# Gate products and two weight sums of the first stage on GpSimd, and a younger head's scalings behind an older head's states

## The chip, the core and the metric

The kernel runs on one core of a Trainium2 chip. Five engines work side by side, each through its own queue in order: TensorE (matrix products, PE in the profile), VectorE (DVE), ScalarE (ACT), GpSimd (POOL) and SyncE (SP, which issues most of the DMAs). GpSimd issues some DMAs itself. An instruction that waits holds up everything behind it on its engine.

The metric is the device time of one execution in microseconds (us): 2118.82 us as the median of three runs of the kernel before (2116.53, 2118.82 and 2120.09).

## What is computed

The reference is a decoder trunk of two layers over 1024 tokens of width 1024. A mixer and a squared-ReLU MLP alternate, each followed by a layer norm. The second layer's mixer is a convolution, which the change does not touch. The first layer's mixer, HGRN2, is a gated linear recurrence with eight heads of 128 channels:

```python
proj = h @ w_in                       # columns [q | forget | value | output gate]
q, fz, v, g = jnp.split(proj, 4, axis=-1)
q = silu(q);  f = lb + (1 - lb) * sigmoid(fz);  k = 1 - f
# per head: S_t = diag(f_t) S_{t-1} + k_t v_t^T ,  o_t = S_t^T q_t
o = o * rsqrt(mean(o * o) + eps) * norm_g
o = o * silu(g)                       # the gate product
mix = o @ w_out
```

## The kernel before

All products are in float32 by splitting each operand into a high part (a rounded copy that ScalarE makes) and a low part (operand less high part, on VectorE), and by three matmuls for high-high, high-low and low-high. The large products use a scheme with seven products of half-size blocks in place of eight (a form of Strassen's), so their operands are sums and differences of blocks. One such product with its operands is called a form here, with the numbers 1, 2, 6, 5, 7, 3, 4 in the order in which they are computed.

**First stage.** After the value columns (up to about 90 us) come the columns of q, forget and gate. They are taken in 12 pairs of 128-column blocks (`PAIRS`, line 37): eight pairs hold q and forget of one head, four hold the gates of two heads. A pair has seven forms, and `pair_product` (line 815) makes each with twelve matmuls in four groups of three. Each group ends with a call of `slot` (line 842), so a form has four slots. `later(n, job)` (line 353) puts a job off by n slots: it is emitted, in the order of its call, when `tick` (line 359) reaches that slot. So the order of the work on every engine is written out by hand by these counts of slots; no scheduler moves anything.

**Weight sums.** `make_form` (line 543) prepares the weight side of one form some four forms ahead of its product. A pair's four weight blocks b0 to b3 (tiles `pr`, of which there are five) are loaded by SP (`load_block`, line 536, DMA at line 541). Four sums of 128x512 make the other operands, in place, all on VectorE: b0 := b0+b2 behind form 2 (line 565), total := b0+b3 in form 6 (line 557), b1 := b1+total in form 6 (line 558, used by form 3), and b2 := b2+b3 in form 5 (line 560, used at once by form 5). `high` (line 570) has ScalarE copy the operand into the tile `fs` (line 571 in the profile), and `low` (line 562) has VectorE make the low part. For forms 6 and 5 the copy is put off by one slot, so that the sum has time (line 574). When a block has been used for the last time its tile is free, and `load_block` issues the next load into it.

**Recurrences.** `recurrence(h)` (line 591) is a generator of eighteen steps for one head; `step` (line 827) advances every active head by one step, older first, about every four slots. Steps 1 to 6 have no matmul: they clamp the forget gate (`f`), multiply cumulative products into q and k (`scale`, line 606, written as qk<-qk,T in the profile), take a reciprocal and make a second copy of k and q with it (`kd`, line 632 on ScalarE and line 634 on VectorE). Steps 7 to 11 form the scores inside chunks of 128, with a scaling and a masked copy put off by one slot behind each. Step 13 transposes k on TensorE, and ScalarE copies it one slot later to `kt` (line 668). Steps 14 and 15 form the outer products of kt and the values; one slot later `chain` (line 718) makes the running states with four small VectorE operations for each half, and `attend` (line 727) of the next step reads them on TensorE. `settle` (line 675) then sums squares, has GpSimd make the root (lines 680 and 474), and steps 17 and 18 transpose the result, scale it and store it to DRAM (line 706, `od`). The next head becomes active when the older one has done nine steps (`LAG`), so steps 1 to 6 of the younger head run beside steps 10 to 15 of the older one.

**Gates.** `gate_turn` (line 851) runs at each slot. It has SP load a head's half from `od` into one of two tiles `u` (line 856), and when the gate of that half is made and the load is nine slots old, VectorE multiplies the two (line 861, t<-u,t in the profile, twelve times; the last two heads are handled by `last_in`, line 904). Two slots later SP stores the product to `zd` (line 864).

**Beside it.** GpSimd's queue in this stage holds the small root operations and `block_sums` (line 368), which prepares weight sums of a later stage in DRAM: per call two plain DMAs (lines 375 and 376), then three accumulating ones (lines 377 and 379), each of which waits for the landing of the one it builds on.

Of the kernel before, what the change touches and what calls it, by code (L numbers as in the profile page):

```python
# [12 lines left out]
ALU = mybir.AluOpType  # L13
# [224 lines left out]
def body(ctx, tc, d, out):  # L238
    nc = tc.nc
# [9 lines left out]
    def view(kb, shape, dt=F32, name="t"):  # L249
        at, top = int(kb * 1024), KBYTES * 1024  # L250
        if at < edge[0]:
            if edge[0] < top:
                space.tile([P, (top - edge[0]) // 4], F32, name="gap")
            edge[0] = 0
        if at > edge[0]:
            space.tile([P, (at - edge[0]) // 4], F32, name="gap")
        edge[0] = at + (prod(shape) + 7) // 8 * 32
        return space.tile([P, *shape], dt, name=name)
# [34 lines left out]
    vector = Clocked(nc.vector, bg.dve, vector_cost)  # L293
# [59 lines left out]
    def later(n, job):  # L353
        if n:
            waiting.append((ticks[0] + n, job))
        else:
            job()
# [175 lines left out]
    total = view(122, wide_t, F32, "total")  # L533
    made, blocks_of, at_block, at_form = [], {}, [0], [0]

    def load_block():
        p, b = divmod(at_block[0], 4)
        if p < len(PAIRS) and free:
            at_block[0] += 1
            raw = blocks_of[p, b] = free.pop(0)  # L540
            nc.sync.dma_start(out=raw, in_=d["wp"][p, b])

    def make_form(wait=1):
        p, i = divmod(at_form[0], 7)
        if p == len(PAIRS):
            return
        at_form[0] += 1
        i, b, s = ORDER[i], [blocks_of.get((p, k)) for k in range(4)], fs()
        hi, lo = s[:, 0], s[:, 1]
        made.append(s)  # L550

        def plus(out, x, y):
            vector.tensor_tensor(out=out, in0=x, in1=y, op=ALU.add)

        raw = total if i == 6 else b[{1: 0, 2: 1, 5: 2, 7: 0, 3: 1, 4: 3}[i]]
        if i == 6:
            plus(total, b[0], b[3])
            plus(b[1], b[1], total)
        elif i == 5:
            plus(b[2], b[2], b[3])  # L560

        def low():
            vector.tensor_tensor(out=lo, in0=raw, in1=hi.bitcast(F32), op=ALU.subtract)
            if i == 2:
                plus(b[0], b[0], b[2])
            if i in (5, 7, 3, 4):
                free.append(raw)
                load_block()

        def high():  # L570
            nc.scalar.copy(out=hi, in_=raw)
            later(wait, low)

        later(wait if i in (6, 5) else 0, high)

    level_ps, out_ps = (banks[:, k : k + 2].rearrange("p k (a b) -> p (k a) b", b=P) for k in (3, 5))
    state_ps = banks[:, 7].rearrange("p (a b) -> p a b", b=P)
# [2 lines left out]
    def mul(o, a, b):  # L580
        vector.tensor_tensor(out=o, in0=a, in1=b, op=ALU.mult)
# [169 lines left out]
    recs, active, pace, alone = [], [], [0.0, 0.0], [False]  # L751
# [75 lines left out]
    def step():  # L827
        if recs and (not active or len(active) == 1 and active[0][2] >= LAG):
            active.append([recs[0], recurrence(recs.pop(0)), 0])
        if not active:  # L830
            return False
        if not (len(active) == 1 and active[0][0] == H - 1 and active[0][2] >= LAG):
            alone[0] = not alone[0]
            if alone[0]:
                return True
        for one in list(active):
            one[2] += 1
            if next(one[1], one) is one:
                active.remove(one)
        return True  # L840

    def slot():
        tick()
        gate_turn()
        pace[0] += pace[1]
        if pace[0] >= 1:
            pace[0] = pace[0] - 1 if step() else 0.0
# [3 lines left out]
    def gate_turn():  # L851
        now = ticks[0]
        if to_load and len(loaded) < 2 and done.get(to_load[0], now) <= now - 7:
            at = to_load.pop(0)
            u = p1("u")
            nc.sync.dma_start(out=u, in_=od[at[0]][at[1]])
            loaded.append((at, u, now))
        if loaded and loaded[0][0] in gates and loaded[0][2] <= now - 9:
            (h, half), u, _ = loaded.pop(0)
            g = gates.pop((h, half))  # L860
            mul(g, u, g)

            def store():
                nc.sync.dma_start(out=zd[half][:, h, :], in_=g)
                stored[h, half] = ticks[0]

            later(2, store)

    oT, ws = [None, None], [[None] * 4, [None] * 4]

# [52 lines left out]
    for _ in range(5):  # L923
        load_block()
    v_products(3, [lambda: cut_v(4, a3), make_form, make_form])
    v_products(4, [make_form])
    fs.views.append(view(160, (2, HT), F32R, "fs"))
# [13 lines left out]
    for i in range(2):  # L941
        load_values(i)

    make_form()
    tick(4)
    for p, (kind, j) in enumerate(PAIRS):
        st = {"banks": dict(turn_of)}
        turn_of = {"z": turn_of["a"], "a": turn_of["b"], "b": turn_of["z"]}
        pace[1] = 0.0 if p == 0 else 0.6 if p < 3 else 0.5
        if kind == "g" and p < len(PAIRS) - 1:  # L950
            to_load += [(2 * j, 0), (2 * j + 1, 1), (2 * j, 1), (2 * j + 1, 0)]
        if p == len(PAIRS) - 1:
            seam()
        for i in ORDER:
            if kind == "q" and i == 2:
                while any(a[0] <= j - 3 for a in active) or recs and recs[0] <= j - 3:
                    tick()
                    step()
            pair_product(p, i, made.pop(0), st)
            later(2, make_form)  # L960
            if (7 * p + ORDER.index(i)) % 6 == 1 and len(to_sum) > 4:
                block_sums(*to_sum.pop(0), gap=12)
        if kind == "q":
            later(4, lambda j=j: recs.append(j))
# [8 lines left out]
    while step():  # L973
        tick()
# [21 lines left out]
    def gain(kb, name, layer):  # L996
        return vec(kb, f"{name}_g", layer), vec(kb + 4, f"{name}_b", layer)
# [75 lines left out]
    g, b = gain(192, "ln_mix", 0)  # L1073
    y = [view(160 + 16 * h, (NTB, D), F32, "y") for h in range(2)]
# [253 lines left out]
    y = [view(32 + 16 * h, (NTB, D), F32, "y") for h in range(2)]  # L1328
    fw = Slots(nc, vector, slots([112, 120, 144, 152, 128, 136, 168], "dw"), raws([192, 196, 200, 204, 160, 164], "dr"), spare, 5, range(12, 56))
    fh = Slots(nc, vector, slots([0, 8, 16, 24, 96, 104, 176], "dh"))  # L1330
    g, b = gain(184, "ln_ffn", 0)
# [236 lines left out]
    y = ct  # L1568
    g, b = gain(120, "ln_ffn", 1)
# [87 lines left out]
```

## Time and profile before

| | us |
|---|---|
| median of three runs | 2118.82 |
| the profiled execution | 2120.82 |
| its span on the core | 2119.0 |
| TensorE busy in the span | 2086.5 |
| VectorE busy | 1447.1 |
| ScalarE busy | 1037.4 |
| GpSimd busy | 390.0 |

The profile is of one execution. Its views are: the page (busy time of each engine over the span); the busy time by windows (a row has the window, its length, the busy us of PE, PE's weight loads, DVE, ACT and POOL with counts of instructions, then the granted TensorE clock as a share of full speed, the DMA share and GB/s); the waits (engine, the tile it was about to write and the line, what released it, us in total, number, longest); the timeline of an engine (start us, us, engine, line, operation, out<-in, shape, count; in brackets the idle time before it and who ended it); groups of instructions (line, engine, operation, tiles, shapes, count | busy us, mean ns | idle us before); and the chain of waits, which follows the work that ended last back through what released each piece. Matmuls and most vector operations are emitted by helper lines and all stand at line 173, so they are told apart by their tiles.

### The profile page before, as it was taken

The page shows a single profiled execution, that of the slowest core. Times are in us where ns is not written, and L with a number is a line of the kernel's source. Part 1 is how long each engine was busy: PE and PEld are TensorE (multiplying, and loading weights), DVE is VectorE, ACT ScalarE, POOL GpSimd, SP SyncE. Part 2 cuts the span into 40 slices and gives each one's busy share as a digit, 9 for nine tenths or more (in the row PEclk, how much of TensorE's full clock was granted, in tenths as well). Part 3 has the DMA queues.
Part 4 walks back from the last instruction along what each step waited for, and adds up shares of the span by engine and source line. Part 5 has one row for each costly group of instructions (what it writes and reads, how often), then busy time and mean ns, then how long its engine had stood idle before and what let it go on. Part 6 is the DMA issues. An engine that isn't in the chain of part 4 may idle for free.

```text
span 2119.0 us, 27037 instructions
## 1 busy us (share of the span) xinstructions
PE 2086.5 (98%) x10056; PEld 1731.7 (82%) x10056; DVE 1447.1 (68%) x1868; ACT 1037.4 (49%) x1593; POOL 390.0 (18%) x384
## 2 busy tenths in 40 slices
PE   8999999999999999999999999999999999999998
PEld 7888787888888888888888888888878888888887
DVE  8697788877775665665666997899436443654456
ACT  5445454541465555544444677378443443433333
POOL 0112212201000000000002897299001000000001
PEclk9999999999999999999999999999999999999999
DMA  4778889771589786989997654564694987855542
GB/s 182 235 176 212 234 226 243 191 257 70 170 256 316 261 280 226 365 327 336 350 335 285 265 193 184 210 256 150 190 334 159 353 308 288 327 204 190 196 161 100
DMA packets 173494, 508.62 MB, mean 240 GB/s; under 512 B 16433, under 2 KB 45361, under 8 KB 172337
## 3 DMA queue, kind: packets, MB, share of 16 engines
q1 hardware_dynamic: 157872, 448.16, 59.0%
q0 software_dynamic: 15488, 58.72, 12.1%
q8 instruction: 79, 1.29, 0.2%
q14 instruction: 55, 0.44, 0.1%
HBM read 377.32 MB, written 196.61 MB: 271 GB/s over the span
## 4 chain that ended last, share of the span: by engine, by line
PE 78%; DVE 9%; DMA 6%; POOL 3%; issue 2%; ACT 2%; SPq 0%; DVEq 0%; POOLq 0%; ACTq 0%
PE ps L173 78%; POOL cb L173 3%; DVE qk L173 2%; DMA wa<-ready 1%; DMA raw<-in_w_dram 1%; DVE t L173 1%; DMA y<-kept 1%; DVE fs L173 1%; DMA vr<-in_wv_dram 1%; DMA hf<-ht 1%; DMA raw<-in_w1q_dram 1%; DVE xf L173 1%; DVE at L173 0%; DMA dh<-hf 0%; DVE vr L173 0%
## 5 line engine op out<-in xcount | busy, mean ns | idle before, releaser
L173 PE MATMUL ps<-dw,dh 128*128 128x512 f32 x2688 | 611.3, 389 | 0.0
L173 PEld LDWEIGHTS ps<-dw,dh 128*128 128x128 f32 x2688 | 504.1, 188 | 104.9 <-ACT dh L70 0.5
L173 PE MATMUL ps<-x1f,fw 128*128 128x512 f32 x1344 | 308.5, 390 | 1.1 <-DVE c L173 0.9
L173 PEld LDWEIGHTS ps<-x1f,fw 128*128 128x128 f32 x1344 | 251.2, 188 | 54.0 <-issue 1.3
L173 PE MATMUL ps<-xa,wa 128*128 128x512 f32 x1152 | 268.8, 392 | 0.0
L173 PE MATMUL ps<-xf,fs 128*128 128x512 f32 x1008 | 251.1, 400 | 1.7 <-ACT t L781 0.8
L173 PEld LDWEIGHTS ps<-xa,wa 128*128 128x128 f32 x1152 | 214.2, 188 | 43.5
L173 POOL TENSOR_TENSOR cb<-cb,prod 128x512 f32<-128x512 f32 x176 | 234.6, 1342 | 17.5 <-ACT prod L1425 7.0
L173 PEld LDWEIGHTS ps<-xf,fs 128*128 128x128 f32 x1008 | 185.6, 190 | 40.2 <-DVE t L173 2.2
L173 DVE TENSOR_TENSOR dh<-dh 128x1024 fp32r<-128x1024 f32 x112 | 136.4, 1222 | 114.5 <-ACT dh L70 113.8
L173 DVE TENSOR_TENSOR dw<-dr,dw 128x1024 fp32r<-128x1024 f32 x112 | 136.6, 1222 | 105.6 <-ACT dw L70 105.0
L173 DVE SCALAR_TENSOR_TENSOR ps<-u,par,ps 128x512 f32<-128x512 f32 x288 | 198.6, 748 | 9.9 <-ACT ps L1437 8.5
L70 ACT CAST dh<-dh 128x1024 fp32r<-128x1024 f32 x112 | 117.0, 1050 | 146.5 <-DMA dh<-hf 146.0
L70 ACT CAST dw<-dr 128x1024 fp32r<-128x1024 f32 x112 | 117.4, 1053 | 135.9 <-PE ps L173 124.5
L173 PE MATMUL ps<-xc,wa 128*128 128x512 f32 x768 | 174.4, 389 | 0.0
L474 POOL TENSOR_TENSOR mv<-mv,nhalf 128x1 f32<-128x1 f32 x32 | 45.2, 1414 | 686.3 <-DVE mv L173 686.3
L173 PEld LDWEIGHTS ps<-xc,wa 128*128 128x128 f32 x768 | 144.1, 188 | 29.9
L1425 ACT ACTIVATE prod<-u,par 128x512 f32<-128x512 f32 x176 | 125.4, 722 | 54.3 <-POOL cb L173 53.7
L173 DVE TENSOR_TENSOR wa<-raw,wa 128x1024 fp32r<-128x1024 f32 x51 | 66.5, 1306 | 67.9 <-ACT wa L70 67.8
L70 ACT CAST wa<-raw 128x1024 fp32r<-128x1024 f32 x51 | 53.6, 1050 | 117.5 <-PE ps L173 109.6
L1288 POOL COPY next<-ss 128x1 f32<-128x1 f32 x37 | 17.3, 467 | 410.9 <-DVE spare L173 259.6
L173 PE MATMUL ps<-w,oT 128*128 128x512 f32 x384 | 89.2, 391 | 0.8 <-ACT oT L872 0.8
(198 smaller groups left out, 2685.4 us busy)
## 6 DMA issues: line engine op xcount, KB each, us to landing
wa<-ready SPq DMA_DIRECT2D x122, 512.0 KB, 4.2
dh<-hf SPq DMA_DIRECT2D x112, 512.0 KB, 5.2
sum_w<-in_w_dram POOLq DMA_DIRECT2D x40, 1024.0 KB, 10.8
ready<-spare SPq DMA_DIRECT2D x74, 512.0 KB, 4.9
dr<-sum_w SPq DMA_DIRECT2D x64, 512.0 KB, 4.5
raw<-in_w_dram SPq DMA_DIRECT2D x51, 512.0 KB, 4.4
dr<-in_w_dram SPq DMA_DIRECT2D x48, 512.0 KB, 5.1
raw<-in_w1q_dram SPq DMA_DIRECT2D x36, 512.0 KB, 4.6
```

The lines of the kernel that those rows point to most:

```text
L70: self.nc.scalar.copy(out=slot[:, 0, c], in_=raw[:, c])
L173: return op(*args, **kw)
L474: nc.gpsimd.tensor_tensor(out=dst, in0=src, in1=nhalf[:, :n], op=ALU.pow)
L1288: nc.gpsimd.tensor_copy(out=raw[:, :1], in_=now)
L1425: nc.scalar.activation(tp, u[:, k : k + HT], AF.Copy, scale=tap(j, k))
```

## The change

It has three parts, all in the first stage:

- Of the four weight sums of a pair, b1+total and b2+b3 go to GpSimd. b2+b3 is no longer made in form 5 but behind form 2, right after b0+b2. Form 5's copy on ScalarE is no longer put off by a slot.
- In `step`, a head that is not the oldest active one takes its first six steps one slot later than before, behind the jobs that the older head had put off to that slot.
- The gate product in `gate_turn` goes to GpSimd, and its store is issued four slots later instead of two.

```diff
-        def plus(out, x, y):
-            vector.tensor_tensor(out=out, in0=x, in1=y, op=ALU.add)
+        def plus(out, x, y, engine=vector):
+            engine.tensor_tensor(out=out, in0=x, in1=y, op=ALU.add)
 
         raw = total if i == 6 else b[{1: 0, 2: 1, 5: 2, 7: 0, 3: 1, 4: 3}[i]]
         if i == 6:
             plus(total, b[0], b[3])
-            plus(b[1], b[1], total)
-        elif i == 5:
-            plus(b[2], b[2], b[3])
+            plus(b[1], b[1], total, nc.gpsimd)
 
         def low():
             vector.tensor_tensor(out=lo, in0=raw, in1=hi.bitcast(F32), op=ALU.subtract)
             if i == 2:
                 plus(b[0], b[0], b[2])
+                plus(b[2], b[2], b[3], nc.gpsimd)
...
-        later(wait if i in (6, 5) else 0, high)
+        later(wait if i == 6 else 0, high)
...
         for one in list(active):
             one[2] += 1
-            if next(one[1], one) is one:
-                active.remove(one)
+
+            def go(one=one):
+                if next(one[1], one) is one:
+                    active.remove(one)
+
+            later(1 if one is not active[0] and one[2] <= 6 else 0, go)
         return True
...
             g = gates.pop((h, half))
-            mul(g, u, g)
+            nc.gpsimd.tensor_tensor(out=g, in0=u, in1=g, op=ALU.mult)
...
-            later(2, store)
+            later(4, store)
```

## The prediction

> **What bounds the kernel now.** I read the page first, then the engines' busy time in the stage that the diff touches and in all that follows it. The stretch from 95 to 445 us holds the pair products of the first stage with the eight recurrences between them; its end is the first product of the output projection.
>
> ```profile
> span 2119.0 us, 27037 instructions
> ...
> PE 2086.5 (98%) x10056; PEld 1731.7 (82%) x10056; DVE 1447.1 (68%) x1868; ACT 1037.4 (49%) x1593; POOL 390.0 (18%) x384
> ```
> ```profile
> 95.00:445.00 350.00, 336.85 (x2188) 286.29 (x2186) 290.30 (x433) 169.04 (x400) 68.25 (x86) 0.99 0.83 222
> ```
> ```profile
> 445.00:2119.00 1674.00, 1660.83 (x7492) 1373.88 (x7492) 1087.56 (x1338) 820.55 (x1122) 314.98 (x284) 1.00 0.70 246
> ```
> TensorE sets the time: 336.85 us busy of 350 in the stage, 1660.83 of 1674 behind it. So the change can win at most the stage's idle 13.15 us and what the clock lost (0.99), and a microsecond won there is won at the end, since the rest runs as it did. VectorE is the second engine in the stage, 290.3 of 350 us (83%). Next come the stage's waits:
>
> ```profile
> POOL sum_w L379 <- DMA sum_w<-in_w_dram: 83.6, 9, 11.7
> ...
> ACT fs L571 <- DVE pr L173: 24.9, 10, 4.4
> ...
> PE ps L173 <- ACT kt L668: 4.7, 3, 4.0
> PE ps L173 <- DVE state L173: 4.0, 3, 2.6
> ```
> Two kinds of waits make 8.7 of TensorE's 13.15 idle us: for the turned keys kt (line 668) and for the states (line 724). Each is mostly one long stop (longest 4.0 and 2.6). TensorE's timeline shows them:
>
> ```profile
> 233.05 0.49 PE L173 MATMUL ps<-state,qk 128*128 128x128 f32 x2 [2.62 <-DVE state L173]
> ```
> ```profile
> 320.77 0.49 PE L173 MATMUL ps<-state,qk 128*128 128x128 f32 x2 [1.16 <-DVE state L173]
> ```
> ```profile
> 359.69 1.55 PE L173 MATMUL ps<-v,kt 128*128 128x128 f32 x8 [3.96 <-ACT kt L668]
> ```
> The two long stops also cost clock right behind them (the eighth number of a row is the granted clock, 1.00 at full speed):
>
> ```profile
> 230.00:235.00 5.00, 2.38 (x17) 2.19 (x17) 4.74 (x9) 0.25 (x2) 0.00 (x0) 0.90 0.65 210
> 235.00:237.00 2.00, 2.00 (x8) 1.78 (x8) 0.90 (x3) 1.40 (x9) 0.92 (x2) 0.50 0.46 131
> ...
> 320.00:324.00 4.00, 3.23 (x22) 3.02 (x23) 3.21 (x9) 1.50 (x9) 0.00 (x0) 1.00 0.98 328
> ...
> 360.00:362.00 2.00, 2.00 (x11) 1.81 (x10) 1.80 (x4) 1.16 (x3) 0.00 (x0) 0.58 1.08 297
> 362.00:364.00 2.00, 2.00 (x7) 1.56 (x6) 1.97 (x2) 0.00 (x0) 0.00 (x0) 0.57 0.97 187
> ```
> Lost at 233: 0.10 x 5 + 0.50 x 2 = 1.5 us; at 360: 0.42 x 2 + 0.43 x 2 = 1.7 us. The stop of 1.16 us left the clock at 1.00.
>
> **What caused the stops.** At 359.69 it is ScalarE's queue:
>
> ```profile
> 357.27 0.62 ACT L571 CAST fs<-pr 128x512 fp32r<-128x512 f32 x1 [3.66 <-DVE pr L173]
> 357.79 1.04 ACT L632 COPY kd<-qk 128x1024 f32<-128x1024 f32 x1
> 358.74 0.90 ACT L668 COPY kt<-ps 128x896 f32<-128x896 f32 x1
> ```
> The copy of form 5 stood 3.66 us for the sum b2+b3 on VectorE, and behind it stood the younger head's copy kd and then kt, for which TensorE waited. At 233.05 it is VectorE's queue:
>
> ```profile
> 227.32 0.68 DVE L173 TENSOR_TENSOR pr<-pr 128x512 f32<-128x512 f32 x1
> 227.91 0.69 DVE L173 TENSOR_TENSOR t<-u,t 128x512 f32<-128x512 f32 x1
> ...
> 229.72 0.68 DVE L173 TENSOR_TENSOR t<-u,t 128x512 f32<-128x512 f32 x1
> 230.32 1.22 DVE L173 TENSOR_TENSOR kd<-qk,rt 128x1024 f32<-128x1024 f32 x1
> 231.57 1.22 DVE L173 TENSOR_TENSOR qk<-qk,T 128x1024 f32<-128x1024 f32 x1
> 232.71 0.28 DVE L173 COPY state<-ps 128x128 f32<-128x128 f32 x1
> ```
> Ahead of the older head's first state stand one sum, two gate products and two scalings of the younger head (kd, qk<-qk,T).
>
> **The order, part by part.** (1) A younger head's first six steps are emitted one slot later, behind what the older head put off by one slot: its states, its scaling, the copy kt. None of these six steps issues a matmul, so TensorE's order stays. (2) b2+b3 is emitted in form 2's second half, two forms before its copy, and that copy loses its wait of a slot. (3) That sum, b1+total and the twelve gate products go to GpSimd, and a gate's store is issued four slots behind instead of two. Worked out:
> - Stop at 359.69: the sum is made two forms earlier and kd follows kt, so both causes go: 3.96 + 1.7 = 5.7 us. At the worst the copy waits for GpSimd instead (a rival below).
> - Stop at 233.05: 0.68 + 2 x 0.69 + 1.22 + 1.22 = 4.5 us leave the queue ahead of the state. The two products still run then, on GpSimd, and may hold VectorE up by 1.29 us each (below), 2.6 us. The state comes 1.9 to 4.5 us earlier; I take 2.0 of 2.62, by the end with the full hold. The 0.6 us left is less than the 1.16 that cost no clock, so 1.5 us goes too: 3.5 us.
> - Stop at 320.77: the same two scalings, 2.4 us, leave, and two sums may hold it up: 0.9 of 1.16. The other two waits for kt are 4.7 - 3.96 = 0.7 us, and kd's 1.04 us leaves its place ahead of kt: 0.7.
>
> Together 5.7 + 3.5 + 0.9 + 0.7 = 10.8 us. Bounds: nothing, if the waits only move on, and 13.15 + 3.2 = 16.3 us, if all idle time and clock loss went.
>
> The Trainium skill's "TensorE: Matmul & The Clock Gate" (Why this matters for your kernels) puts the fall of the clock at gaps above about 3 us. By it the gap of 2.62 us would cost no clock and the sum were 1.5 us less; the row at 235 us differs (0.50), and I go by it.
>
> **What GpSimd takes and gives back.** VectorE loses 12 x 0.685 + 12 x 0.692 + 12 x 0.684 = 24.7 us (of the 24 pr<-pr, the twelve b2+b3 move):
>
> ```profile
> L173 DVE TENSOR_TENSOR pr<-pr 128x512 f32<-128x512 f32 x24 | 16.4, 685 | 0.0
> ...
> L173 DVE TENSOR_TENSOR pr<-pr,total 128x512 f32<-128x512 f32 x12 | 8.3, 692 | 0.4
> ...
> L173 DVE TENSOR_TENSOR t<-u,t 128x512 f32<-128x512 f32 x12 | 8.2, 684 | 0.1
> ```
> The nearest row for the same operation on GpSimd is that of the convolution, 1.34 us; beside it VectorE's split of wa, with two inputs in SBUF, is stretched, against 1.22 us where GpSimd is quiet:
>
> ```profile
> L173 POOL TENSOR_TENSOR cb<-cb,prod 128x512 f32<-128x512 f32 x176 | 234.6, 1342 | 17.5 <-ACT prod L1425 7.0
> ```
> ```profile
> 1447.87 1.94 DVE L173 TENSOR_TENSOR wa<-raw,wa 128x1024 fp32r<-128x1024 f32 x1
> ...
> 1453.02 1.78 DVE L173 TENSOR_TENSOR wa<-raw,wa 128x1024 fp32r<-128x1024 f32 x1
> ...
> 1459.06 2.10 DVE L173 TENSOR_TENSOR wa<-raw,wa 128x1024 fp32r<-128x1024 f32 x1 [0.30 <-ACT wa L70]
> ```
> ```profile
> L173 DVE TENSOR_TENSOR wa<-raw,wa 128x1024 fp32r<-128x1024 f32 x34 | 41.5, 1223 | 51.6 <-ACT wa L70 51.5
> ```
> The three lost 0.72, 0.56 and 0.88 us. They read like an operation that waits until GpSimd's has ended; the bound of one hold is then a product's own undisturbed time, near 1.29 us (an estimate from the 1.34 mean, which has stretched ones in it). In the first stage most of VectorE's operations have two inputs in SBUF, so I take the high end of the three, 0.86: 36 x 0.86 = 31 us against 24.7 saved, so VectorE has 6.3 us more. Bounds: no hold, -24.7; full hold, 36 x 1.29 = 46.4, so +21.7. What of it reaches TensorE I take from the chain of waits in the stage:
>
> ```profile
> by line: PE ps L173 59.0%; DVE qk L173 11.8%; issue 5.3%; DVE t L173 4.5%; DVE fs L173 4.3%; DVE at L173 2.9%; DVE rt L173 2.4%; DVE pr L173 2.1%; DVE T L173 1.9%; DVE kd L173 1.3%; DVE f L173 1.2%; DVE total L173 0.9%; ACT fs L571 0.5%; AC
> ```
> VectorE's lines are 33% of it: 6.3 x 0.33 = 2.1 us lost (bounds -8 and +7 by the same share, +21.7 if all arrives).
>
> The Trainium skill speaks against moving work this way: "SBUF — State Buffer" (Who interferes with whom) says that a VectorE instruction with two SBUF inputs contends with a GpSimd instruction that reads SBUF, and that the second to issue blocks fully. The stretched rows agree. With every product a full hold the sum were +21.7 us for VectorE instead of +6.3.
>
> **The queue of GpSimd and of SP.** GpSimd runs in order, and its accumulating DMAs (line 379) wait up to 11.7 us for the one before. A sum behind such a wait is late, and with it ScalarE's copy. In the program's order the two sums of the eighth pair stand between these two rows of GpSimd, and ScalarE's copy is the third:
>
> ```profile
> 282.60 1.03 POOL L474 TENSOR_TENSOR ss<-ss,nhalf 128x4 f32<-128x4 f32 x1
> 291.57 0.91 POOL L379 DMA_DIRECT2D sum_w<-sum_w  x1 [7.95 <-DMA sum_w<-in_w_dram]
> ```
> ```profile
> 292.35 0.62 ACT L571 CAST fs<-pr 128x512 fp32r<-128x512 f32 x1 [2.85 <-DVE pr L173]
> ```
> GpSimd is free at 283.6, 8.7 us before the copy, and two products take 2.6. I looked at all twelve pairs in the same way; most have 10 us or more. So I cost the queue at nothing; the cover is this lead, and without it a late sum stops ScalarE as at 357 us. The gate's store on SP waits for a product twice as long, two slots later; behind it stand loads of pr. The stage's 84 products have four slots each, 336 in 350 us, so a slot is about a microsecond, and a gate's product may start some 2.7 us late (four slots less 1.3) before SP waits for it. The block sums themselves are wanted long after the stage.
>
> **Sum.** 10.8 - 2.1 = 8.7 us. The profiled execution took 2120.82 us (span 2119.0 and 1.8 around it); it would take 2112.1. It was 2.0 us above the median 2118.82, so the median falls to 2110.1: 2110.
>
> **The rivals.**
> - *The stall moves on.* The removed waits come back as waits for the next scaling or for PSUM. For it: the chain names many VectorE lines and only 59% TensorE. Against: the two long stops have causes of their own, each now out of the queue. About 2 us won: 2117. This is also the case that the change does not do what it says.
> - *The hold decides (slower).* Each product holds VectorE by its full time where VectorE has no slack, and TensorE waits. For it: 83% busy and the stretched rows. Against: a third of the chain, not all. Price: 21.7 - 10.8 = 10.9 us more, 2130. It beats the gain from (24.7 + 10.8) / 36 = 0.99 us a product, all passed on.
> - *GpSimd's queue decides.* A DMA wait of 11.7 us ahead of a sum, with two products, is 14.3 - 8.7 = 5.6 us of ScalarE, 7.3 with the clock. Two such events, 14.6 against 8.7: 2125. Against: the leads above.
>
> **How the numbers follow.** Forecast 0.58 (2105 to 2114.5); stall moves on 0.20; hold 0.14; queue 0.08. A change within 0.2% (4.2 us: 2114.6 to 2123.1) can't be told from none here. Faster: 0.58 and a share of the second case, 0.62. Within: the rest of that case and the light ends of the last two, 0.22. Slower: 0.16. The range takes the forecast, below it part of the bound of 16.3 us, above it the second case and the light ends: 2104 to 2122.
>
> **What would show it.** Right: no stop over 2 us for kt or state between 95 and 445 us, no wait of ScalarE's fs copy for a sum, granted clock 1.00 throughout, TensorE idle there of 5 to 8 us, fs and qk operations of VectorE stretched beside GpSimd's products, VectorE busy within 6 us or so of 290. Wrong: waits for pr on GpSimd, for qk<-qk,T over a microsecond, or new stops above 2.6 us.

## The result and the profile after

| | before | after |
|---|---|---|
| median, same chip, six runs each | 2117.68 us | 2128.31 us |
| lowest and highest | 2116.35 to 2120.26 | 2123.21 to 2130.67 |
| the profiled execution | 2120.82 | 2127.28 |

The ratio is 1.0046, with a 95% interval from 1.0033 to 1.0060: the change costs 9.7 us (0.0046 x 2118), where 8.7 were forecast as won. The page of after, and the stage up to the first product of the output projection, which stood at 445.48 us before:

```profile
span 2125.5 us, 27085 instructions
...
PE 2088.2 (98%) x10056; PEld 1735.8 (82%) x10056; DVE 1443.3 (68%) x1832; ACT 1036.8 (49%) x1593; POOL 441.8 (21%) x420
```
```profile
454.57 0.73 PE L173 MATMUL ps<-w,oT 128*128 128x512 f32 x2 [0.80 <-ACT oT L875]
```
```profile
95.00:454.50 359.50, 340.26 (x2183) 289.00 (x2181) 286.56 (x399) 169.08 (x400) 120.00 (x123) 0.98 0.82 219
```
The stage ends 454.57 - 445.48 = 9.1 us later. TensorE is idle in it for 359.50 - 340.26 = 19.2 us; before it was 13.6 (the window from 95 to 445.4 had 350.4 us, 336.85 of them busy). So 5.7 us are idle time. The rest is clock: before, two stops cost it 3.2 us, and after it is four.

```profile
230.00:240.00 10.00, 7.32 (x36) 6.58 (x36) 9.86 (x12) 3.50 (x13) 3.85 (x4) 0.83 0.97 179
290.00:300.00 10.00, 9.18 (x51) 8.42 (x52) 4.97 (x8) 6.39 (x13) 4.44 (x5) 0.83 0.75 164
360.00:370.00 10.00, 6.96 (x27) 5.32 (x26) 9.78 (x14) 4.46 (x8) 5.79 (x6) 0.83 0.82 278
420.00:430.00 10.00, 8.14 (x49) 7.24 (x48) 7.41 (x10) 5.98 (x13) 7.75 (x6) 0.87 0.73 168
```
10 x (0.17 + 0.17 + 0.17 + 0.13) = 6.4 us (the last of the four drops runs on a little past 430 us), 3.2 more than before. 5.7 + 3.2 = 8.9 of the 9.1 us. VectorE has less to do than before (286.56 us against 290.70 in those two windows), so it isn't its load that lengthens the stage. It is where its work stands and when it is done. TensorE's timeline has the stop ahead of each of the four, and one at 222.57 that cost no clock:

```profile
222.57 3.02 PE L173 MATMUL ps<-xf,fs 128*128 128x512 f32 x12 [1.61 <-DVE t L173]
...
236.10 0.61 PE L173 MATMUL ps<-state,qk 128*128 128x128 f32 x2 [2.68 <-DVE state L173]
...
290.82 1.05 PE L173 MATMUL ps<-ident,f 128*128 128x128 f32 x4 [1.86 <-ACT f L684]
...
366.12 4.11 PE L173 MATMUL ps<-xf,fs 128*128 128x512 f32 x10 [3.01 <-ACT t L780]
...
426.65 2.63 PE L173 MATMUL ps<-kd 128*128 128x128 f32 x14 [1.86 <-DVE at L173]
```
The stop for kt is gone, and ScalarE's copy of fs waits no more for a sum on VectorE but for 1.7 us in all (24.9 before). In their place GpSimd waits, and the normalised heads f wait for GpSimd (3.4 us before, the longest 0.8):

```profile
POOL pr L553 <- DVE pr L173: 70.5, 8, 14.5
DVE qk L173 <- PE ps L173: 38.1, 22, 3.3
...
ACT f L684 <- POOL ss L474: 10.5, 8, 4.0
...
ACT fs L570 <- DVE total L173: 1.7, 3, 0.7
```

**The stop at 236.10.** VectorE's and GpSimd's timelines:

```profile
228.23 1.23 DVE L173 TENSOR_TENSOR fs<-total,fs 128x512 fp32r<-128x512 f32 x1 [0.74 <-ACT fs L570]
229.39 3.46 DVE L173 TENSOR_TENSOR t<-t,sq 128x512 f32<-128x512 f32 x1
...
235.78 0.27 DVE L173 COPY state<-ps 128x128 f32<-128x128 f32 x1
```
```profile
228.86 0.89 POOL L379 DMA_DIRECT2D sum_w<-sum_w  x1
229.47 1.50 POOL L377 DMA_DIRECT2D sum_w<-in_w_dram  x1
230.23 2.06 POOL L864 TENSOR_TENSOR t<-u,t 128x512 f32<-128x512 f32 x1
```
The two scalings no longer stand ahead of the state. But an instruction of 0.68 us lasts 3.46: it is held from before the gate's product begins to half a microsecond after its end, through the issue of a transfer and the product behind it.

**The stop at 290.82.** GpSimd's queue, then ScalarE's:

```profile
287.02 1.20 POOL L377 DMA_DIRECT2D sum_w<-in_w_dram  x1 [5.71 <-issue]
288.30 0.19 POOL L679 TENSOR_SCALAR ss<-ss 128x4 f32<-128x4 f32 x1
288.57 1.02 POOL L474 TENSOR_TENSOR ss<-ss,nhalf 128x4 f32<-128x4 f32 x1
```
```profile
289.62 1.14 ACT L684 ACTIVATE f<-ps,ss 128x128 f32<-128x128 f32 x4 [3.07 <-POOL ss L474]
```
The small root operations stand behind a transfer that was issued only at 287.02, 5.71 us after GpSimd had become idle; ScalarE and then TensorE wait for the root. By the program's order that transfer builds on a plain one (line 375), which GpSimd issued at 272.48, 9.9 us later than before the change (262.63). Before, the same transfer was issued at 279.04, and the root behind it ran at 282.32 without waiting for it.

**The stop at 222.57.** VectorE's timeline:

```profile
220.62 0.17 DVE L173 COPY dec<-T 128x8 f32<-128x8 f32 x1
220.69 1.23 DVE L173 TENSOR_TENSOR qk<-qk,f 128x1024 f32<-128x1024 f32 x1
221.82 0.69 DVE L173 SCALAR_TENSOR_TENSOR t<-t,ps 128x512 f32<-128x512 f32 x1
```
The younger head's first scaling, qk<-qk,f, now stands between the older head's dec and the evacuation t<-t,ps. The evacuation empties the PSUM bank that TensorE waits for: ready at 222.51, TensorE goes on at 222.57.

**The stop at 366.12** is both together. ScalarE's copy kd waits for a scaling of 1.22 us that took 2.28 beside a gate's product (362.04, 1.38 us), and the evacuation t<-ps stands behind kd:

```profile
364.54 1.05 ACT L631 COPY kd<-qk 128x1024 f32<-128x1024 f32 x1 [2.64 <-DVE qk L173]
365.49 0.58 ACT L780 COPY t<-ps 128x512 f32<-128x512 f32 x1
```

**The stop at 426.65** stands behind held instructions. Ahead of the masked copy `at`, for which TensorE waits, two of VectorE's small products, of 0.22 and 0.18 us, last 1.31 and 1.28 us while GpSimd makes sums and gate products, and the low part of total takes 1.21 us instead of 0.69:

```profile
418.00 1.31 DVE L173 TENSOR_TENSOR T<-T 128x64 f32<-128x64 f32 x1
...
422.33 1.28 DVE L173 TENSOR_TENSOR T<-T 128x32 f32<-128x32 f32 x1
...
425.27 1.32 DVE L173 COPY_PREDICATED at<-mask,ps 128x1024 f32<-128x1024 int32 x1
```
The same stop, 1.83 to 1.88 us and the clock behind it, is in the traces of r5, r13 and r15 below, with GpSimd's transfers there or not, and not in those of r4 and r14, which have no products on GpSimd.

How much was held: the groups of GpSimd's products, from 60 to 460 us (line, operation, count | busy us, mean ns | idle before), and two of VectorE's that were stretched, from 95 to 455 us (691 and 682 ns before):

```profile
L864 POOL TENSOR_TENSOR t<-u,t 128x512 f32<-128x512 f32 x12 | 18.2, 1513 | 19.5 <-DVE t L173 10.7 <-PE ps L173 7.5 <-DVE T L173 1.4
L553 POOL TENSOR_TENSOR pr<-pr 128x512 f32<-128x512 f32 x12 | 18.0, 1497 | 154.6 <-DVE pr L173 142.3 <-DMA od<-kt 10.0 <-DVE T L173 2.3
...
L553 POOL TENSOR_TENSOR pr<-pr,total 128x512 f32<-128x512 f32 x12 | 16.1, 1345 | 13.4 <-ACT sq L764 12.6 <-DVE total L173 0.8
```
```profile
L173 DVE TENSOR_TENSOR fs<-total,fs 128x512 fp32r<-128x512 f32 x11 | 12.4, 1132 | 10.5 <-ACT fs L570 10.5
...
L173 DVE TENSOR_TENSOR t<-t,sq 128x512 f32<-128x512 f32 x11 | 10.3, 938 | 0.1
```
"Stretch" below is, from 60 to 470 us, the sum over all of VectorE's instructions of the duration less the median of the same instruction (operation, tiles, shape) in r4_vector, where GpSimd makes no product. It is -0.2 us for before and 17.8 us for after, 0.49 for each of the 36 products.

### The profile page after: what moved, and what is told of

It is laid out like the page before. It is cut to its first block, busy times and chain, and to the rows that moved or that the text cites. A ratio compares the mean times of both kernels' runs of the same rounds, so it can differ in the third digit from the quotient of the medians.

```text
span 2125.5 us, 27085 instructions
## 1 busy us (share of the span) xinstructions
PE 2088.2 (98%) x10056; PEld 1735.8 (82%) x10056; DVE 1443.3 (68%) x1832; ACT 1036.8 (49%) x1593; POOL 441.8 (21%) x420
## 4 chain that ended last, share of the span: by engine, by line
PE 83%; DVE 6%; DMA 4%; POOL 3%; issue 2%; ACT 2%; SPq 0%; DVEq 0%; POOLq 0%; ACTq 0%
PE ps L173 83%; POOL cb L173 2%; DVE qk L173 2%; DMA raw<-in_w_dram 1%; DMA wa<-ready 1%; DMA sum_w<-in_w_dram 1%; DVE fs L173 1%; DVE t L173 1%; DVE at L173 0%; DVE T L173 0%; DVE wa L173 0%; DVE rt L173 0%; DVE ps L173 0%; ACT prod L1428 0%; DMA back<-zd 0%
## 6 DMA issues: line engine op xcount, KB each, us to landing
sum_w<-in_w_dram POOLq DMA_DIRECT2D x40, 1024.0 KB, 10.3
```

## The experiments

Every kernel stands against the kernel before on its own chip. The last column is (ratio - 1) x 2118.

| kernel | what it is | median us | ratio, 95% interval | us |
|---|---|---|---|---|
| after | the whole change | 2128.31 | 1.0046 [1.0033, 1.0060] | +9.7 |
| r1_order | steps 1 to 6 later, alone | 2115.64 | 0.9984 [0.9975, 0.9992] | -3.4 |
| r2_sums | two sums on GpSimd, alone | 2122.66 | 1.0016 [1.0008, 1.0025] | +3.4 |
| r3_gates | gate products on GpSimd, alone | 2119.41 | 1.0007 [0.9998, 1.0016] | +1.5 |
| r9_order_sums | the first two | 2121.05 | 1.0016 [1.0007, 1.0024] | +3.4 |
| r10_order_gates | order and gates | 2118.20 | 0.9999 [0.9990, 1.0008] | -0.2 |
| r12_sums_gates | sums and gates | 2122.79 | 1.0022 [1.0013, 1.0032] | +4.7 |
| r4_vector | after, all on VectorE | 2116.74 | 0.9987 [0.9979, 0.9996] | -2.8 |
| r5_nodma | after, GpSimd's transfers out | 2120.11 | 1.0005 [0.9997, 1.0014] | +1.1 |
| r6_nodma_vector | r4, GpSimd's transfers out | 2116.58 | 0.9987 [0.9978, 0.9996] | -2.8 |
| r7_dummy_add | r4 with 72 idle adds on GpSimd | 2135.26 | 1.0085 [1.0072, 1.0099] | +18.0 |
| r8_dummy_set | r4 with 72 memsets on GpSimd | 2117.63 | 0.9993 [0.9984, 1.0002] | -1.5 |
| r11_order46 | steps 4 to 6 later, alone | 2111.70 | 0.9969 [0.9957, 0.9981] | -6.6 |
| r13_after46 | after, but steps 1 to 3 in place | 2119.15 | 0.9997 [0.9988, 1.0006] | -0.6 |
| r14_46_early | r11 with b2+b3 early on VectorE | 2112.48 | 0.9966 [0.9953, 0.9978] | -7.2 |
| r15_after46_nodma | r13, GpSimd's transfers out | 2111.64 | 0.9968 [0.9955, 0.9980] | -6.8 |
| r16_behind | r4, 72 adds behind transfers | 2143.50 | 1.0112 [1.0085, 1.0139] | +23.7 |
| r17_ahead | r4, 72 adds ahead of transfers | 2136.59 | 1.0076 [1.0056, 1.0095] | +16.1 |

### The parts alone, and two by two

r1_order:

```diff
-            if next(one[1], one) is one:
-                active.remove(one)
+            def go(one=one):
+                if next(one[1], one) is one:
+                    active.remove(one)
+            later(1 if one is not active[0] and one[2] <= 6 else 0, go)
```


> Only the younger head's later steps; all sums and gate products stay on VectorE. Theory A (work on GpSimd costs the time, by its holds on VectorE and by its queue): this part alone wins what was predicted for the stops at kt and the states, 3 to 9 us, ratio 0.996 to 0.9985. Theory B (the later order itself costs it, since a younger head's operations now stand ahead of PSUM evacuations and the copy kd ahead of one): slower by 2 to 8 us, ratio 1.001 to 1.004.

r2_sums:

```diff
-            plus(b[1], b[1], total)
+            plus(b[1], b[1], total, nc.gpsimd)
...
-        elif i == 5:
-            plus(b[2], b[2], b[3])
...
+                plus(b[2], b[2], b[3], nc.gpsimd)
...
-        later(wait if i in (6, 5) else 0, high)
+        later(wait if i == 6 else 0, high)
```


> Only the two sums on GpSimd, b2+b3 made early; order of the heads and gates as before. Theory A: slower by 3 to 9 us (24 products, longest waits where a sum stands behind a DMA issue on GpSimd or where a root stands behind a sum). Theory B: 0 to 5 us faster, since ScalarE's copy no longer waits for the sum.

r3_gates:

```diff
-            mul(g, u, g)
+            nc.gpsimd.tensor_tensor(out=g, in0=u, in1=g, op=ALU.mult)
...
-            later(2, store)
+            later(4, store)
```


> Only the gate products on GpSimd, their store at four slots. Theory A: slower by 1 to 5 us (12 products). Theory B: within 2 us of before.

r9_order_sums, r10_order_gates and r12_sums_gates are the same hunks in pairs.

> Later steps of the younger head and the sums on GpSimd, gates on VectorE. Additive theory (each part costs what it cost alone: -2.7 and +4.3 us): 2119 to 2121. Interaction theory (the sums on GpSimd cost more in the new order, since the younger head's operations now stand at VectorE's tight places beside them): 2122 to 2127.

> Later steps of the younger head and the gate products on GpSimd, sums on VectorE. Additive theory: 2116 to 2118 (-2.7 and +1.1 us). Interaction theory: 2119 to 2123.

> All 36 operations on GpSimd, the heads in the order of before. Additive theory: +4.3 and +1.1 us, 2123 to 2125. Interaction between order and GpSimd: the same 2121 to 2125, and the changed kernel's further 4 us come from the order. If sums and gates get in each other's way in GpSimd's queue: 2126 to 2130.

Only the order wins (3.4 us). Neither move to GpSimd wins by itself, though each takes work from VectorE: the sums cost 3.4 us, and the gates' 1.5 us can't be told from nothing. The stretch is 11.7 us in r2_sums and 3.7 in r3_gates. Alone the three make -3.4 + 3.4 + 1.5 = +1.5 us, together +9.7. Order and gates show nothing beyond their sum (-0.2 against -1.9, inside the intervals), and neither do sums and gates (4.7 against 4.9). Order and sums do to some extent (3.4 against 0.0). Of the excess of 8.2 us (9.7 less 1.5) the three pairs make 3.4 + 1.7 - 0.2 = 4.9, and 3.3 are left that only all three together show; with these intervals the split is a rough one.

In r1_order ScalarE's copy of fs still waits 3.54 us for the sum on VectorE, and TensorE 3.67 us for kt behind it. So the late sum, which the prediction named, is what makes the stop at 359.69; moving the scalings and kd alone doesn't remove it (r14_46_early below makes the sum early, and the stop is gone).

### The engine, by the same order

r4_vector against after (the order of emission is after's, only the engine differs):

```diff
-            plus(b[1], b[1], total, nc.gpsimd)
+            plus(b[1], b[1], total)
...
-                plus(b[2], b[2], b[3], nc.gpsimd)
+                plus(b[2], b[2], b[3])
...
-            nc.gpsimd.tensor_tensor(out=g, in0=u, in1=g, op=ALU.mult)
+            mul(g, u, g)
```


> The changed kernel's order with nothing on GpSimd: later steps of the younger head, b2+b3 made early, store at four slots, but all 36 operations on VectorE. Theory A: 4 to 11 us faster than before, ratio 0.995 to 0.998, and the 366 us stop (ScalarE's kd ahead of an evacuation) small. Theory B: slower than before by 2 to 8 us, near the changed kernel.

2116.74 us: GpSimd as the engine costs 9.7 + 2.8 = 12.5 us, more than the whole loss. The 2.8 us won fall short of the 4 to 11 of theory A; the order isn't all gain either (below).

r7_dummy_add and r8_dummy_set: r4 with two GpSimd instructions, which nobody waits for, at each of the 36 places where after has a product. The adds read SBUF (128x256, 1.15 us on the mean), the memsets only write it (0.41 us):

```diff
+    def extra():
+        for k in range(2):
+            nc.gpsimd.tensor_tensor(out=dummy[0].rearrange("p (a b) -> p a b", b=P), in0=mask[:, 0:2], in1=mask[:, 1:3], op=ALU.add)
```
```diff
+            nc.gpsimd.memset(dummy[0], 0.0)
```


> r4_vector plus 72 GpSimd additions of 128x256 (two at each of the 36 places), which read a constant and write a scratch tile that nobody uses. Nothing leaves VectorE. Hold theory: 4 to 12 us slower than r8_dummy_set, VectorE's operations with two inputs in SBUF stretched. Queue theory: within 2 us of r8_dummy_set, since nobody waits for them.

> r4_vector plus 72 GpSimd memsets of 128x256 into the same scratch tile at the same places: they take GpSimd's time but read nothing. Both theories: within 2 us of r4_vector (2116.7), no stretched VectorE operation.

The adds cost 18.0 + 2.8 = 20.8 us with a stretch of 22.7, more than the 4 to 12 us expected; the memsets 1.3 us, inside the intervals, with a stretch of 0.3. VectorE's groups in r7_dummy_add, then in r8_dummy_set:

```profile
L173 DVE TENSOR_TENSOR fs<-pr,fs 128x512 fp32r<-128x512 f32 x72 | 52.8, 734 | 16.4 <-ACT fs L579 16.4
L173 DVE TENSOR_TENSOR pr<-pr,total 128x512 f32<-128x512 f32 x12 | 10.7, 892 | 0.4
```
```profile
L173 DVE TENSOR_TENSOR fs<-pr,fs 128x512 fp32r<-128x512 f32 x72 | 49.1, 682 | 15.3 <-ACT fs L579 15.3
L173 DVE TENSOR_TENSOR pr<-pr,total 128x512 f32<-128x512 f32 x12 | 8.3, 692 | 0.4
```
So a hold of VectorE reaches the end by itself, with no queue waiting for the product, and here nearly whole: 20.8 of 22.7 us. The adds also fill GpSimd's queue for longer than the memsets do, but the roots aren't later for it: ScalarE waits 5.0 us for them in r7_dummy_add, 5.3 in r4_vector and 6.8 in r8_dummy_set. The forecast's share was a third.

### GpSimd's transfers out of the queue

r5_nodma against after, and r6_nodma_vector against r4_vector: the block sums of the later stage become two plain copies that SP issues. The twelve later weight sums are left out.

```diff
-                block_sums(*to_sum.pop(0), gap=12)
+                plain_copy(*to_sum.pop(0))
```


> The changed kernel with GpSimd's sixty DMAs taken out of the first stage: each call of the block sums there is two plain copies of 1 MB on SP, so twelve of the later weight sums are left out. Queue theory (what costs 11.6 us against the same order on VectorE is that products and roots on GpSimd stand behind its DMAs, and hold VectorE for longer there): within 4 us of r6_nodma_vector. Hold theory (each product takes VectorE's second input for its time, wherever it stands): still 8 to 12 us slower than r6_nodma_vector.

> The control for r5_nodma: the order of r4_vector with all 36 operations on VectorE, and the same plain copies in place of GpSimd's DMAs (twelve of the later weight sums left out). Both theories: 2110 to 2120 us, near r4_vector, since nothing in the first stage waits for those sums.

With the products on VectorE the transfers cost nothing (-2.8 and -2.8), so it is not their traffic. With the products on GpSimd they cost 9.7 - 1.1 = 8.6 us. The stretch changes little (17.8 to 16.1); the instruction of the long hold at 229.39 takes 1.77 us in r5_nodma, and TensorE waits for f for 0.4 us at most.

The two traces show where the time is. The stage ends at 445.27 us in r5_nodma, 9.3 earlier than in after. The stop for the state is 1.00 us there instead of 2.68 and costs no clock, which is 1.7 + 1.7 = 3.4 us; the stop for f is gone, 1.9 + 1.7 = 3.6 us. The stop behind kd is as long as in after (3.00 us at 358.35), yet the clock stays at 1.00 behind it, another 1.7 us, for which the traces show no reason.

### Steps 4 to 6 alone

r11_order46 against before:

```diff
+            later(1 if one is not active[0] and 4 <= one[2] <= 6 else 0, go)
```


> No work on GpSimd; only steps 4 to 6 of the younger head one slot later, steps 1 to 3 as before. If the 1.6 us stop at 221 us in r1_order (an evacuation of PSUM behind the younger head's first scaling) is due to steps 1 to 3, it goes, and the kernel takes 2111 to 2115, less than r1_order (2115.6) and than both kernels. If not, it is within 1 us of r1_order or slower.

2111.70 us, ratio 0.9969: this beats both kernels, and is 3.2 us better than r1_order. Its stage and VectorE at the place of after's stop at 222.57:

```profile
95.00:445.00 350.00, 341.03 (x2220) 290.29 (x2219) 295.00 (x439) 174.78 (x415) 72.38 (x88) 1.00 0.85 230
```
```profile
217.93 0.17 DVE L173 COPY dec<-T 128x8 f32<-128x8 f32 x1
218.00 0.70 DVE L173 SCALAR_TENSOR_TENSOR t<-t,ps 128x512 f32<-128x512 f32 x1
```
The evacuation follows dec at once, the scaling has been done before, and there is no stop. TensorE is idle for 8.97 us of the window, against 13.15 before. The stop at 233.05 is down to 0.91 us (at 230.27). One long stop is left, 3.02 us for kt at 352.78.

r13_after46 is after with the same line: steps 1 to 3 back in place, everything else as in after. r15_after46_nodma takes GpSimd's transfers out as well (twelve later weight sums left out). r14_46_early is r11 with b2+b3 in form 2's second half, as in after, but on VectorE:

```diff
-            later(1 if one is not active[0] and one[2] <= 6 else 0, go)
+            later(1 if one is not active[0] and 4 <= one[2] <= 6 else 0, go)
```
```diff
-        elif i == 5:
-            plus(b[2], b[2], b[3])
...
+                plus(b[2], b[2], b[3])
...
-        later(wait if i in (6, 5) else 0, high)
+        later(wait if i == 6 else 0, high)
```


> Kernel after, but of the younger head's steps only 4 to 6 are emitted behind the older head's states; steps 1 to 3 stay where they were before the change, all GpSimd work as in after. Theory A (the loss that only the parts together show comes through steps 1 to 3, whose evacuation stands behind the first scaling next to held VectorE instructions): 2117 to 2122, near the sum of steps 4 to 6 alone (-6) and of sums and gates together (+4.7). Theory B (it comes through GpSimd's queue, where products stand between transfers, whatever order the scalings have): 2125 to 2129, with a stop near 236 us behind a held VectorE instruction and one near 290 us behind ScalarE's f.

> As r13_after46, with GpSimd's transfers of this stage taken out of its queue (the twelve later weight sums are left out, as in r5_nodma). If both the queue and steps 1 to 3 cost, each on its own: 2113 to 2117, some 4 to 7 under r5_nodma's 2120.1. If the queue alone makes the interaction, no less than 2119.

> Steps 4 to 6 alone later (2111.7 when run by itself), and the two weight sums b2+b3 emitted early, on VectorE. Theory: the last stop of that kernel, 3.0 us at 352.78 waiting for ScalarE's kt, stands behind ScalarE's copy of fs, which waits for the sum; with the sum early it goes: 2107 to 2110. Rival: the early sum delays the states on VectorE by its 0.69 us each time and another stop takes its place: 2111 to 2114.

r13 (2119.15) came out as its theory A, though the stop behind a held instruction that theory B named is there (3.29 us at 233.21); r15 (2111.64) lower than its expectation; r14 (2112.48) as its rival. The stop for kt went in r14, and another took its place:

```profile
356.25 0.49 PE L173 MATMUL ps<-state,qk 128*128 128x128 f32 x2 [1.50 <-DVE state L173]
```
The early sum is worth nothing that can be measured here (-7.2 against -6.6). Together these kernels make a table of us against before:

| products on | GpSimd's transfers | steps 1 to 6 later | steps 4 to 6 later | cost of steps 1 to 3 |
|---|---|---|---|---|
| VectorE | there | -2.8 (r4) | -7.2 (r14) | 4.4 |
| VectorE | out | -2.8 (r6) | not run | |
| GpSimd | there | +9.7 (after) | -0.6 (r13) | 10.3 |
| GpSimd | out | +1.1 (r5) | -6.8 (r15) | 7.9 |

Each entry has an interval of some 2 to 3 us to either side. (r4 and r6 also store the gate products two slots later than r14; r1 against r11, without that difference, gives 3.2 us for steps 1 to 3.) From r15 to after: steps 1 to 3 cost 7.9 us, the queue with its transfers 8.6, and -6.8 + 7.9 + 8.6 = +9.7. Where neither is there, the move to GpSimd costs next to nothing and wins nothing (r15 against r14: 0.4), with 13.5 us of stretch against the 24.7 us taken off VectorE. This is a net result: r15's trace still has the stop of the holds (1.83 us at 412.14, and the clock behind it), which r14's has not.

One caution: the profiled executions of r13 and r15 differ by 3.7 us in span (2117.4 and 2113.7), less than their ratios (6.2) and medians (7.5) do.

### A product behind a transfer, by itself

In after a product stood behind an issue at 229.47 when VectorE was held for 2.77 us too long, and in r13_after46 the same place has the longest hold of all, 3.40 us (an instruction of 0.28 us):

```profile
226.47 3.68 DVE L173 TENSOR_TENSOR T<-T 128x128 f32<-128x128 f32 x1
```
```profile
226.15 1.29 POOL L377 DMA_DIRECT2D sum_w<-in_w_dram  x1
226.92 3.08 POOL L864 TENSOR_TENSOR t<-u,t 128x512 f32<-128x512 f32 x2
```
In r5 and r15, without transfers, no hold is over 1.11 us. r16_behind and r17_ahead put the 72 idle adds of r7 in pairs behind and ahead of each accumulating transfer:

```diff
-            later((i + 1) * gap, part)
+            later((i + 1) * gap, part if after is not None else (lambda part=part: (part(), extra())))
```


> The kernel of r4_vector (after's order, all sums and gate products on VectorE) with two GpSimd adds of 128x256 that nobody waits for emitted right behind each of the accumulating transfers of the stage, so as many adds as in r7_dummy_add. Theory: an add queued behind a transfer's issue holds a two-input VectorE instruction already while GpSimd still issues, 0.9 to 1.3 us before the add itself runs; then the stretch of VectorE's instructions is clearly over that of r17_ahead (by 10 to 30 us if a third or more of the transfers meets one) and single 0.68-us instructions last 3 us and more. Rival: only the add's own time holds; then both kernels have the same stretch, near r7_dummy_add's 22.9 us, and no instruction is held for longer than two adds.

> The same adds at the same places, emitted ahead of each accumulating transfer instead of behind it. Theory and rival alike: a stretch of 15 to 25 us, as the adds run while the transfer behind them has yet to wait for its data; the transfers are each about 1.3 us later. By the theory r16_behind is slower than this kernel, by the rival the two agree within 3 us.

The theory misses: the stretch is 31.9 us behind and 31.1 ahead, both over the 15 to 25 us expected ahead and the 22.7 of r7_dummy_add with as many adds. That difference stays unexplained. Behind there are four holds over 1.3 us instead of one, the longest 1.43. r16 is slower than r17 as the theory had it (by 7.6 us, with intervals that overlap a little), but not through longer holds: its trace has a stop of 2.32 us for f at 298.33, which r17's has not. The root came late there too:

```profile
291.78 1.23 POOL L377 DMA_DIRECT2D sum_w<-in_w_dram  x1 [1.78 <-issue]
292.54 2.40 POOL L548 TENSOR_TENSOR dum<-mask 128x256 f32<-128x256 f32 x2
295.03 0.51 POOL L686 TENSOR_SCALAR ss<-ss 128x4 f32<-128x4 f32 x1
```
So of the queue's cost of 6 to 9 us, late roots are one part by the traces, and single long holds at one place another (2.75 us also in r12_sums_gates, 2.10 in r10_order_gates). The traces of after and r5_nodma give them about equal shares (3.6 and 3.4 us, above). No kernel was run with the roots on another engine, so this is read from two traces and not tested.

## Why the prediction was wrong

It forecast 2110.0 and faster at 0.62; measured is 2128.31, outside the range, and slower. By its own steps:

- **The cause of the stops** was read rightly: r1_order keeps the sum late and keeps the stop for kt, r11_order46 takes the two scalings from ahead of the state and shrinks the stop at 233.05 to 0.91 us, and r14_46_early makes the sum early and has no stop for kt.
- **"Stop at 359.69: both causes go: 5.7 us."** The wait for kt went and the time didn't. In after the next thing late at this place is the evacuation behind kd (3.01 us at 366.12), in r14 the state (1.50 us). The early sum by itself is worth 0.6 us, which can't be told from nothing. This is the first rival, the stall that moves on, and it held for the largest term of the sum.
- **"Stop at 233.05: 3.5 us."** The scalings' share was right, and r11 has it. But the two products were charged 2.6 us of hold spread over the state's way, where one hold alone took 2.77 us and the stop stayed at 2.68.
- **Part (1) of the order, all six steps as pure gain.** This step failed outright. The text asked what the steps leave (the state's queue, kt's place) and, since they issue no matmul, not what they now stand ahead of: a PSUM evacuation. Steps 1 to 3 cost 3.2 to 4.4 us where VectorE runs undisturbed and 8 to 10 us beside held instructions. Steps 4 to 6 alone win 6.6.
- **The hold.** 0.86 us a product was assumed, 0.49 measured, so VectorE has less to do and not 6.3 us more. The size erred to the safe side. What failed is the price of a hold, the share of 0.33 from the chain of waits: r7 passed on 20.8 of 22.7 us (0.9), r17 18.9 of 31.1 (0.6). A share of the chain is a mean over the stage. Work taken off VectorE earned nothing that can be measured (r15 against r14), and the engine had slack (38.1 us of waiting for TensorE ahead of its qk instructions alone); holds cost where they fell. So the time saved and the time added should not have been netted.

The Trainium skill's "SBUF — State Buffer" (Who interferes with whom) says that a VectorE instruction with two SBUF inputs contends with a GpSimd instruction that reads SBUF, not with one that only writes. The adds of r7 (734 ns against 682) and the memsets of r8 (682) agree with both halves.

- **"So I cost the queue at nothing; the cover is this lead."** This step failed as well: 6.2 to 8.6 us. The lead was counted for the sums alone, from GpSimd's idle time to ScalarE's copy. What stands behind the sums was left out: the transfers, which come later when a sum waits for VectorE (70.5 us in all), and the root operations behind those, for which ScalarE waits 10.5 us instead of 3.4. The gates' products were not asked what they stand behind. The rival "GpSimd's queue decides" (2125) had the right engine, by another wait than the one it named: not a late sum, but late roots and products. "The hold decides" (2130) is nearest to 2128.31, by luck: it had VectorE held for 46.4 us, where 17.8 were measured, and without the transfers and steps 1 to 3 the holds that are left (13.5 us in r15) cost nothing on balance.
- **The clock.** That stops of the size left over cost none rested on one stop of 1.16 us. Four stops of 1.86 to 3.01 us cost 6.4 us in after, while stops of 3.00 and 3.29 us in r5_nodma and r13_after46 cost none (last section), so a stop's length doesn't price it.

The table above settles the sign: without steps 1 to 3 and without the transfers in the queue the change wins 6.8 us (r15), which is what steps 4 to 6 win alone (6.6).

## What to carry to other kernels

When an instruction is moved down a queue, name what it now stands ahead of, evacuations of PSUM first; here half a reordering won 6.6 us, and the other half gave back 3 to 4 of them alone and 8 to 10 beside the moved work. An engine's own queue is part of the price of moving work to it: count not only when the moved work is done but what stands behind it (here the roots behind transfers behind sums), and where it holds another engine. Busy time taken from an engine with slack was worth nothing that could be measured here, while holds in the same engine reached the end by up to nine tenths of their length, so the two are not to be netted through an average.

## What the hardware showed that was not expected

- The length of TensorE's stop doesn't decide whether the granted clock falls. After the stop of 1.86 us at 290.82 in after it was 0.53 for 2.2 us and 0.77 for the next 3, a loss of 1.7 us; after 1.17 and 1.61 us (358.92 and 222.57) it stayed at 1.00:

```profile
222.50:225.00 2.50, 2.43 (x11) 2.02 (x12) 2.50 (x6) 0.63 (x1) 1.20 (x1) 1.00 0.82 329
...
290.80:293.00 2.20, 2.18 (x11) 2.18 (x12) 0.59 (x1) 2.20 (x5) 1.26 (x2) 0.53 1.02 203
```
But it stayed at 1.00 as well after 1.91 us in r4_vector (159.41), 3.00 us in r5_nodma (358.35) and 3.29 us in r13_after46 (233.21), the last shown here:

```profile
233.20:235.00 1.80, 1.79 (x15) 1.79 (x16) 1.73 (x4) 0.37 (x3) 0.00 (x0) 1.00 1.07 214
235.00:237.00 2.00, 2.00 (x12) 1.65 (x11) 1.97 (x3) 1.29 (x7) 1.05 (x2) 1.00 0.95 307
```
The starts of TensorE's products confirm it: behind that stop they are 0.11 us apart, behind the stop at 236.10 in after, for the same products, 0.21. What else decides is open. The Trainium skill's "TensorE: Matmul & The Clock Gate" (Why this matters for your kernels) advises against gaps above about 3 us; in these traces a gap of 1.83 us was enough (r15_after46_nodma, 412.14) and one of 3.29 us was not.

- Holds fall on small instructions as hard as on large ones: products of 0.18 to 0.29 us on VectorE (T<-T) took 1.3 to 3.7 us when a GpSimd product was under way, the longest where two products ran back to back behind a transfer's issue (226.47 in r13_after46).
